# Half-block loop of an S5 layer: products of eigenvalue powers on VectorE four half blocks later, context rows of the fifth block earlier, two pair steps on VectorE

## The chip, the cores and the metric

The kernel runs on one core of a Trainium2 chip, as one launch. The time is device microseconds for one execution; each kernel is run several times, and the median counts. A profile is one further execution, recorded by the hardware profiler. Its *span* reaches from the first to the last instruction. Engines are called as in the profile's rows: PE (TensorE), PEld (its weight loads), DVE (VectorE), ACT (ScalarE), POOL (GpSimd), SP (SyncE, which here only issues transfers).

## The reference, cut to what matters

One layer (DEPTH is 1) of a backbone: an S5 mixer with a GLU over 1024 latent tokens behind a prefix of 256 context tokens, then a SwiGLU feed-forward, each with RMSNorm and adaLN. All is fp32. The part around the change is the S5 scan:

```python
lam_bar = jnp.exp(lam * jnp.exp(log_step.astype(F32))[:, None])
b_bar = ((lam_bar - 1.0) / lam)[..., None] * lax.complex(b_re, b_im)

def run(u, h0):
    bu = jnp.einsum('lgh,gnh->lgn', u.astype(F32), b_bar)
    bu = bu.at[0].add(lam_bar * h0)
    a = jnp.broadcast_to(lam_bar, bu.shape)
    _, h = lax.associative_scan(_linear_combine, (a, bu), axis=0)
    return jnp.einsum('lgn,ghn->lgh', h, c_mat).real, h[-1]

y_c, h_c = run(u_ctx, jnp.zeros(lam_bar.shape, lam_bar.dtype))
y_l, _ = run(u_lat, h_c)
```

There are 64 groups of 16 channels with 64 complex states each, and two directions. Only the latent rows of the result go on.

## The kernel before

**Chunks and half blocks.** The tokens are cut into chunks of T = 8: 32 chunks of context and 128 of latents, 160 in all. The S5 stage first works out what each chunk adds to the state. It does so in 16 *half blocks* (the loop `for hb in range(16)`, lines 699 to 757). Block b holds eight groups, and a half block is one block in one direction. For a half block the program makes an input matrix (`bl_make`: two products of the chunk's eigenvalue powers `LB` with B, on VectorE or, where `PMUL` says so, on GpSimd), adds the two (`bl_sum`: a DMA that accumulates, issued by GpSimd, from half block 4 on), turns the result on TensorE (`bl_tr`, line 443, with ScalarE's copy in line 446), and multiplies the tokens `U` with it (`sums`, line 584); ScalarE copies the chunk states into `STQ` (lines 590, 592 and 593). The work for later half blocks is spread over the loop: in half block hb, `bl_tr(hb + 2)`, `bl_sum(hb + 5)` and `bl_make(hb + 6)` are issued.

**What is interleaved.** The tokens of a block must be normalised and modulated before `sums` reads them: `rs_lat` (VectorE, table `RSL`), `u_act` (ScalarE, table `UACT`, line 497) and, for the context rows, `u_ctx` (GpSimd, table `UCTX`). `pair(hb - 1)` combines neighbouring latent chunks of the half block before, on GpSimd where `PPAIR` lists it and on VectorE otherwise. `ctx_tree` (VectorE, table `CTREE`) folds the 32 context chunks into one state by four doublings.

**Powers.** `PW` holds the powers 1 to 8 of the eigenvalues. Powers 1, 2, 4 and 8 are made early on VectorE; the other four are complex products, `pw_mul`. `pw_full` (line 386, copy in line 388) turns `PW` into `PWF`, which the products of C with the powers (`cl_ops`, GpSimd, from half block 12 on) read. `KD`, a small table, is made beside the first product.

**After the loop.** The last context tree is followed by `ctx_last` and `scan()`: 32 steps over two chunks and 63 over one, all on VectorE, each step dependent on the step before. GpSimd meanwhile makes the products of C, TensorE the convolution matrices and the outputs of what the scan has finished. Then come the GLU and the feed-forward, which fill the larger part of the time with TensorE.

**Order.** Nothing is scheduled by a planner: each engine executes its instructions in the order in which the Python code issues them (`manual_schedule`), and waits for others by semaphores. Tables such as `PPAIR` and `UCTX` therefore set the order. The helpers `tt`, `stt` and `ts` record all arithmetic, so its rows carry lines 77, 80 and 84 to 86; tiles and shapes tell them apart. In names, `ra`, `rw`, `rxa`, `rxc`, `ru`, `r` and `c` lie in SBUF; `lta`, `ltb`, `lbt`, `tq`, `ltc`, `pv`, `pw`, `pe`, `ut`, `xt` and `prow` lie in PSUM. `PW` and the states are in `ra`, the tokens in `ru`.

Of the kernel before, what the change touches and what calls it, by code (L numbers as in the profile page):

```python
# [24 lines left out]
G = 64  # L25
# [17 lines left out]
def s5_ffn_kernel(tc, a, out):  # L43
    nc = tc.nc
    V, S, E, PE, SY = nc.vector, nc.scalar, nc.gpsimd, nc.tensor, nc.sync
    ctx = ExitStack()
    with ctx:
# [5 lines left out]
        def view(reg, kb, shape, parts=P):  # L53
            off = int(round(kb * 256))
            n = int(np.prod(shape))
            v = reg[:parts, off:off + n]
            if len(shape) > 1:
                names = "abcdef"[:len(shape)]
                v = v.rearrange(f"p ({' '.join(names)}) -> p {' '.join(names)}",
                                **{k: d for k, d in zip(names, shape)})  # L60
            return v
# [3 lines left out]
        RA = region("ra", 80.5)  # L65
# [3 lines left out]
        RW = region("rw", 6)  # L69
# [6 lines left out]
        def tt(o, x, y, op, eng=V):  # L76
            eng.tensor_tensor(out=o, in0=x, in1=y, op=op)  # L77
# [263 lines left out]
        def pw_mul(o, x, y):  # L341

            m = x.shape[1]
            a_, b_ = (view(RA, kb, [m, 2, G]) for kb in (42, 43))
            yr, yi = (bc(bc(y[:, i], 1, 2), 1, m) for i in range(2))
            tt(a_, x, yr, MUL, E)
            tt(b_, x[:, :, ::-1], yi, MUL, E)
            tt(o[:, :, 0], a_[:, :, 0], b_[:, :, 0], SUB, E)
            tt(o[:, :, 1], a_[:, :, 1], b_[:, :, 1], ADD, E)

        LH = view(RXc, 0, [2, 3, G])
        SQ = [LS[:, 0], view(RXa, 7.25, [3, G]), LH[:, 0], LH[:, 1], LS[:, 1]]
# [326 lines left out]
            o = CL[q][:, ri, d]  # L679
            return [lambda: prod(0, o), lambda: prod(1, ct), add]  # L680

        PPAIR = (3, 5, 7, 8, 9, 11, 12, 13, 15)
        UACT = {1: (2, 0, 4), 2: (2, 4, 8), 3: (3, 0, 4), 4: (3, 4, 8)}
        UACT.update({6 + i: (4 + i // 2, 4 * (i % 2), 4 * (i % 2) + 4) for i in range(8)})
        UCTX = {1: 2, 3: 3, 6: 4, 7: 5, 9: 6, 11: 7}
        RSL = {0: 2, 1: 3, 3: 4, 5: 5, 6: 6, 8: 7}
        ADA1 = {0: (0, 1), 1: (2, 3, 4), 2: (5, 6, 7)}
        ADA2 = {10: 12, 11: 14, 12: 16, 13: 18, 15: 22}
# [9 lines left out]
        for hb in range(16):  # L698
# [38 lines left out]
                lb_psum(hb + 6)  # L737
            bl_sum(hb + 5)
            bl_make(hb + 6)
            if hb == 3:  # L740
                pw_mul(PW[:, 2:3], PW[:, 0:1], PW[:, 1])
                tt(KD.rearrange("p q g h -> p (q g) h"), bc(pat, 1, 8), bc(dcol, 2, HC), MUL, E)
            if hb == 4:
                pw_mul(PW[:, 4:6], PW[:, 0:2], PW[:, 3])
                pw_mul(PW[:, 6:7], PW[:, 2:3], PW[:, 3])
            if hb in (6, 8):
                pw_full(hb // 2 - 3)
            if hb == 9:
                cs_load(0)
            if hb == 11:  # L750
# [1009 lines left out]
```

## Time and profile before

| | us |
|---|---|
| median of three runs | 1024.25 (1023.15 to 1025.16) |
| profiled execution | 1022.42, of which span 1020.6 |
| TensorE busy over the span | 961.9 (94%) |
| VectorE busy over the span | 785.5 (77%) |
| GpSimd busy over the span | 766.5 (75%) |
| first and last start of the multiplications of `sums` (line 584) | 40.0 and 121.3 |
| all waits of TensorE on line 584 for GpSimd, 44 to 128 us | 2.6, one time |
| all waits of VectorE for ScalarE on line 593, 44 to 128 us | 5.3, two times |

How to read the rows that follow. A row of the order of time has the start and the duration in us, the engine, the line, the operation, the tile written and the tiles read, the shapes, and how many like instructions the row stands for. In brackets stands the time that the engine idled before it, and what ended that idling. A row of a group of instructions has its count behind an x. Starts are counted from the start of the span. DMA issues have a time to landing of their own.

### The profile page before, as it was taken

The numbers are of one execution on the slowest core, as the hardware profiler recorded it, in microseconds if no ns is written. First come the engines' busy times: TensorE is split into PE (matmuls) and PEld (weight loads), VectorE is DVE, ScalarE is ACT, GpSimd is POOL, SyncE is SP. The second block draws the span as 40 slices with busy tenths as digits, with TensorE's granted clock in tenths as the row PEclk, the third lists the DMA queues.
The fourth block names the chain that finished last, engine by engine and source line by source line (L and its number), as shares of the span: only waits on it lengthen the run. The fifth ranks groups of instructions, "written<-read, shape, count | busy, mean of one in ns | idle before, by whom it ended". The sixth has DMA issues, their size and how long they took to land. (4 is left out here: it accounts for less than half of the span.)

```text
span 1020.6 us, 18545 instructions
## 1 busy us (share of the span) xinstructions
PE 961.9 (94%) x6988; PEld 771.8 (76%) x6988; DVE 785.5 (77%) x1642; ACT 436.5 (43%) x854; POOL 766.5 (75%) x590
## 2 busy tenths in 40 slices
PE   5987798779999999999999999999999999999996
PEld 1466423668999987878888888888888888888885
DVE  7979799994365777997958768585958778686987
ACT  5477622234454663523334343424343343324337
POOL 5799899991682548979786877778686877777674
PEclk9999999989999999999999999999999999999999
DMA  9764997323612021011212112121212111121205
GB/s 335 276 139 91 298 341 231 91 74 89 227 61 83 2 104 62 22 42 42 83 41 74 39 45 62 42 73 52 73 42 82 39 40 58 42 73 52 73 22 165
DMA packets 48546, 98.95 MB, mean 97 GB/s; under 512 B 4285, under 2 KB 18877, under 8 KB 47177
## 3 DMA queue, kind: packets, MB, share of 16 engines
q1 hardware_dynamic: 43272, 86.64, 25.9%
q0 software_dynamic: 2016, 7.34, 3.8%
q10 hardware_dynamic: 3168, 3.79, 1.1%
q8 instruction: 55, 0.90, 0.4%
q14 instruction: 35, 0.28, 0.1%
HBM read 84.25 MB, written 6.17 MB: 89 GB/s over the span
## 5 line engine op out<-in xcount | busy, mean ns | idle before, releaser
L77 POOL TENSOR_TENSOR c<-rxc,c 128x512 fp32r<-128x512 f32 x128 | 170.0, 1342 | 55.6 <-ACT c L1227 53.7
L1286 PE MATMUL ut<-ra,c 128*128 128x512 f32 x400 | 155.8, 390 | 0.5 <-ACT ra L1227 0.3
L1287 PE MATMUL ut<-ra,c 128*128 128x512 f32 x400 | 155.7, 389 | 0.3 <-DVE ra L77 0.3
L1288 PE MATMUL ut<-ra,c 128*128 128x512 f32 x400 | 155.7, 389 | 0.0
L1227 ACT CAST c<-rxc 128x512 fp32r<-128x512 f32 x128 | 79.0, 622 | 146.4 <-PE xt L1568 51.8
L1568 PE MATMUL xt<-c,c 128*128 128x512 f32 x540 | 129.7, 389 | 0.0
L77 DVE TENSOR_TENSOR ru<-ru,xt 128x1024 f32<-128x1024 f32 x90 | 107.8, 1216 | 12.9 <-PE xt L1568 9.1
L1568 PEld LDWEIGHTS xt<-c,c 128*128 128x128 f32 x540 | 101.4, 188 | 21.0
L77 DVE TENSOR_TENSOR ru<-ut,ru 128x512 f32<-128x512 f32 x98 | 67.2, 686 | 42.4 <-PE ut L1288 36.9
L1286 PEld LDWEIGHTS ut<-ra,c 128*128 128x128 f32 x400 | 75.1, 188 | 16.7 <-ACT ra L1227 0.8
L1287 PEld LDWEIGHTS ut<-ra,c 128*128 128x128 f32 x400 | 75.1, 188 | 16.2 <-issue 0.6
L1288 PEld LDWEIGHTS ut<-ra,c 128*128 128x128 f32 x400 | 75.1, 188 | 15.9 <-POOL c L77 0.3
L77 POOL TENSOR_TENSOR c<-rw,c 128x512 fp32r<-128x512 f32 (+1 forms) x29 | 39.8, 1372 | 37.3 <-ACT c L1227 36.6
L77 POOL TENSOR_TENSOR c<-ru,c 128x512 fp32r<-128x512 f32 (+1 forms) x39 | 58.0, 1487 | 9.3 <-ACT c L1227 4.9
L1288 PE MATMUL ut<-c,c 128*128 128x512 f32 x160 | 62.4, 390 | 1.3 <-POOL c L77 1.3
L1287 PE MATMUL ut<-c,c 128*128 128x512 f32 x160 | 62.3, 389 | 0.0
L1286 PE MATMUL ut<-c,c 128*128 128x512 f32 x160 | 62.2, 389 | 0.0
L77 POOL TENSOR_TENSOR rxc<-rxc 128x512 f32<-128x512 f32 x40 | 60.9, 1523 | 1.6
L1568 PE MATMUL ut<-c,c 128*128 128x512 f32 x216 | 51.9, 389 | 0.0
L584 PE MATMUL pv<-ru,c 128*64 128x160 f32 x512 | 43.7, 312 | 7.3 <-POOL ru L77 2.6
L77 DVE TENSOR_TENSOR pe<-pe,ru 128x256 f32<-128x256 f32 x64 | 27.4, 429 | 29.5 <-ACT pe L1127 17.4
L77 DVE TENSOR_TENSOR ru<-ru,ut 128x512 f32<-128x512 f32 x76 | 47.3, 680 | 0.3
(427 smaller groups left out, 2568.2 us busy)
## 6 DMA issues: line engine op xcount, KB each, us to landing
c<-in_ada_w SPq DMA_DIRECT2D x46, 256.0 KB
rxc<-in_w SPq DMA_DIRECT2D x38, 256.0 KB
rxc<-in_w SPq DMA_DIRECT2D x19, 512.0 KB
ru<-in_w SPq DMA_DIRECT2D x11, 512.0 KB
rw<-in_w SPq DMA_DIRECT2D x11, 512.0 KB
ra<-in_ada_w SPq DMA_DIRECT2D x10, 512.0 KB
ra<-in_ada_w SPq DMA_DIRECT2D x18, 256.0 KB
ru<-in_xT SPq DMA_DIRECT2D x4, 1024.0 KB
```

Of the source, the lines that this page charges most:

```text
L77: eng.tensor_tensor(out=o, in0=x, in1=y, op=op)
L584: PE.matmul(pv[64 * (i % 2):64 * (i % 2) + 64, ri, c0:c0 + 160], w[:, i, 64 * ri:64 * ri + 64], U[:, 8 * b + 4 * j + i], start=True, stop= ...
L1227: S.copy(o[0], x)
L1286: PE.matmul(pu, wh, bh, start=start, stop=False)
L1287: PE.matmul(pu, wh, bl, start=False, stop=False)
L1288: PE.matmul(pu, wl, bh, start=False, stop=stop)
L1568: PE.matmul(pd, w[:, cs_], b, start=j in (1, 2, 4) and n == 0, stop=n == 2, skip_group_check=j not in (1, 2, 4))
```

## The change

Three things in the half-block loop are different.

`pw_mul`, the complex product of powers, is issued on VectorE (`V`) instead of GpSimd (`E`). Its two scratch tiles move from `ra` to one in PSUM (`LTb`) and one in SBUF (`RW`). The three calls come four half blocks later, 7 and 8 instead of 3 and 4, and `pw_full` comes in half blocks 9 and 10 instead of 6 and 8; `KD` goes along to half block 7 and stays on GpSimd.

The context rows of the fifth block (`u_ctx(4)`) are issued in half block 5 instead of 6.

Pair steps 8 and 12 leave the list for GpSimd, so VectorE executes them.

```diff
@@ def pw_mul(o, x, y):
             m = x.shape[1]
-            a_, b_ = (view(RA, kb, [m, 2, G]) for kb in (42, 43))
+            a_, b_ = (t[:, :128 * m].rearrange("p (m r n) -> p m r n", m=m, r=2) for t in (LTb, view(RW, 0, [256])))
             yr, yi = (bc(bc(y[:, i], 1, 2), 1, m) for i in range(2))
-            tt(a_, x, yr, MUL, E)
-            tt(b_, x[:, :, ::-1], yi, MUL, E)
-            tt(o[:, :, 0], a_[:, :, 0], b_[:, :, 0], SUB, E)
-            tt(o[:, :, 1], a_[:, :, 1], b_[:, :, 1], ADD, E)
+            tt(a_, x, yr, MUL, V)
+            tt(b_, x[:, :, ::-1], yi, MUL, V)
+            tt(o[:, :, 0], a_[:, :, 0], b_[:, :, 0], SUB, V)
+            tt(o[:, :, 1], a_[:, :, 1], b_[:, :, 1], ADD, V)
...
-        PPAIR = (3, 5, 7, 8, 9, 11, 12, 13, 15)
+        PPAIR = (3,5,7,9,11,13,15)
...
-        UCTX = {1: 2, 3: 3, 6: 4, 7: 5, 9: 6, 11: 7}
+        UCTX = {1: 2, 3: 3, 5: 4, 7: 5, 9: 6, 11: 7}
...
-            if hb == 3:
+            if hb == 7:
                 pw_mul(PW[:, 2:3], PW[:, 0:1], PW[:, 1])
                 tt(KD.rearrange("p q g h -> p (q g) h"), bc(pat, 1, 8), bc(dcol, 2, HC), MUL, E)
-            if hb == 4:
+            if hb == 8:
                 pw_mul(PW[:, 4:6], PW[:, 0:2], PW[:, 3])
                 pw_mul(PW[:, 6:7], PW[:, 2:3], PW[:, 3])
-            if hb in (6, 8):
-                pw_full(hb // 2 - 3)
+            if hb in (9, 10):
+                pw_full((9, 10).index(hb))
```

How the engines' lists change, at three places. The first is on VectorE, at the end of half block 7: the two rows at the top are the last of a context tree, the row of `ru` is the scaling of block 7's tokens.

```order
 L77 TENSOR_TENSOR ra<-ra,ltb 128x16x2x8
 L77 TENSOR_TENSOR ra<-ra,lbt 128x16x2x8
+L77 TENSOR_TENSOR ltb<-ra 128x128
+L77 TENSOR_TENSOR rw<-ra 128x128
+L77 TENSOR_TENSOR ra<-ltb,rw 128x64 x2
 L77 TENSOR_TENSOR ru<-ru,ltb 128x8x128
```

The first product of powers stands ahead of the scaling of block 7. Its two multiplications read `ra` twice.

The second place is on VectorE too, from half block 8 to 9: the rows of `c` are the two products of half block 14; behind the piece follow a context tree and the products of half block 15.

```order
 L77 TENSOR_TENSOR c_63<-c_63,lbt 128x1024
 L77 TENSOR_TENSOR c_66<-c_63,lbt 128x1024
+L77 TENSOR_TENSOR ltb<-ra 128x256
+L77 TENSOR_TENSOR rw<-ra 128x256
+L77 TENSOR_TENSOR ra<-ltb,rw 128x2x64 x2
+L77 TENSOR_TENSOR ltb<-ra 128x128
+L77 TENSOR_TENSOR rw<-ra 128x128
+L77 TENSOR_TENSOR ra<-ltb,rw 128x64 x2
+L77 TENSOR_TENSOR ltb<-ra,lta 128x256
+L77 TENSOR_TENSOR lbt<-ra,lta 128x256
+L77 TENSOR_TENSOR ra<-ra,ltb 128x32x2x4
+L77 TENSOR_TENSOR ra<-ra,lbt 128x32x2x4
```

The other two products of powers, and behind them pair step 8 (the last four rows), stand between the products of half block 14 and those of half block 15.

The third is on GpSimd, from half block 4 to 6: the rows of `c_64` and `rxc` are the two products of half block 10, the DMA is the sum of that half block, and the rows of `ru` are the context rows of the fifth block.

```order
 L77 TENSOR_TENSOR c_64<-c_63,c_65 128x1024
 L77 TENSOR_TENSOR rxc<-c_63,c_65 128x1024
-L77 TENSOR_TENSOR ra<-ra 128x256 x2
-L77 TENSOR_TENSOR ra<-ra 128x2x64 x2
-L77 TENSOR_TENSOR ra<-ra 128x128 x2
-L77 TENSOR_TENSOR ra<-ra 128x64 x2
+L77 TENSOR_TENSOR ru<-ru,r_60 128x8x32 x2
 L433 DMA c_64<-rxc 128x1024
-L77 TENSOR_TENSOR ru<-ru,r_60 128x8x32 x2
 L77 TENSOR_TENSOR rxc<-ra,r_60 128x256 x2
```

Two products of powers are gone from ahead of the DMA, and the context rows pass from behind it to ahead of it.

## The prediction, made before the result was known

> **What bounds the kernel now.** I first read the busy time by stretch, cut where the program's stages meet (columns: stretch, its length, then the busy time of TensorE, its weight loads, VectorE, ScalarE and GpSimd, the granted clock, DMA share, GB/s).
>
> ```profile
> 68.60:90.40 21.80, 18.07 (x180) 14.29 (x180) 20.12 (x55) 15.87 (x35) 21.17 (x33) 0.92 0.48 92
> 90.40:110.40 20.00, 15.70 (x160) 11.88 (x159) 18.87 (x49) 16.53 (x38) 19.53 (x26) 1.00 0.68 154
> 110.40:115.04 4.64, 3.57 (x43) 2.90 (x42) 0.00 (x1) 4.05 (x10) 4.56 (x6) 1.00 1.04 300
> 115.04:122.42 7.38, 6.05 (x69) 4.70 (x66) 5.28 (x20) 5.61 (x13) 7.30 (x9) 1.00 1.03 374
> 127.65:227.56 99.91, 83.63 (x1512) 48.12 (x1504) 97.77 (x509) 26.48 (x56) 96.86 (x66) 0.96 0.59 188
> ```
>
> From 127.65 to 227.56 us VectorE runs the serial scan without a gap (97.77 of 99.91 us), and the stages behind it start from its end. The scan starts 5.23 us after the last context tree, which starts at 122.42 when the loop's last states are copied. So this edit is worth what it does to that 122.42. Inside the loop GpSimd (21.17 of 21.80) and VectorE (20.12 of 21.80) are both full. Next I read VectorE's own order of time for what it still waits for:
>
> ```profile
> 115.04 0.43 DVE L77 TENSOR_TENSOR ltb<-ra,lta 128x256 f32<-128x256 f32 x1 [4.64 <-ACT ra L593]
> 120.20 0.43 DVE L77 TENSOR_TENSOR ltb<-ra,lta 128x256 f32<-128x256 f32 x1 [1.15 <-ACT ra L590]
> 122.42 0.43 DVE L77 TENSOR_TENSOR ltb<-ra,lta 128x256 f32<-128x256 f32 x1 [0.68 <-ACT ra L593]
> ```
>
> Those three gaps, 6.47 us, are all the slack VectorE has between 70 and 122 us apart from 0.4 us. TensorE waits in the same loop. The first of these rows is the wait for the context rows of the fifth block, the second the one for sum 14, the third the last transpose (half block 15); the fourth is ScalarE's copy of the last states, which ends the loop:
>
> ```profile
> 84.57 3.80 PE L584 MATMUL pv<-ru,c 128*64 128x160 f32 x32 [2.60 <-POOL ru L77]
> 109.81 1.06 PE L443 MATMUL pv<-r,c 128*128 128x128 f32 x8 [1.20 <-DMA c<-c]
> 114.40 1.09 PE L443 MATMUL pv<-r,c 128*128 128x128 f32 x8 [1.07 <-ACT ra L593]
> 122.12 0.27 ACT L593 COPY ra<-pv 128x128 f32<-128x128 f32 x1
> ```
>
> The last transpose reads a sum that an accumulating DMA finishes, issued on GpSimd once VectorE has made both products. The rows are VectorE's products, GpSimd's issue, and the landing that the query of that issue gives (minimum, median, maximum of one):
>
> ```profile
> 99.86 2.35 DVE L77 TENSOR_TENSOR c<-c,lbt 128x1024 f32<-128x1024 f32 x2 [0.20 <-ACT ra L590]
> 105.46 0.88 POOL L433 DMA_DIRECT2D c<-c  x1
> DMA to landing us min/median/max: 8.8/8.8/8.8
> ```
>
> 105.46 + 8.8 = 114.26: the transpose took the sum 0.14 us after it landed. Eight microseconds later (122.12 + 0.27 = 122.39) ScalarE has copied the last states. VectorE's products for half block 15 are thus one transfer away from the end of the loop.
>
> **What leaves GpSimd.** These rows, in order: the first product of powers, the other two, the context rows of the fifth block (they stay, earlier), pair step 8 and pair step 12 (two rows each).
>
> ```profile
> 68.61 1.84 POOL L77 TENSOR_TENSOR ra<-ra 128x128 f32<-128x128 f32 x4
> 78.08 4.27 POOL L77 TENSOR_TENSOR ra<-ra 128x256 f32<-128x256 f32 x8
> 82.91 1.60 POOL L77 TENSOR_TENSOR ru<-ru,r 128x256 f32<-128x256 f32 x2
> 99.10 1.30 POOL L77 TENSOR_TENSOR rxc<-ra,r 128x256 f32<-128x256 f32 x2
> 100.36 1.55 POOL L77 TENSOR_TENSOR ra<-ra,rxc 128x256 f32<-128x256 f32 x2
> 112.35 1.29 POOL L77 TENSOR_TENSOR rxc<-ra,r 128x256 f32<-128x256 f32 x2
> 113.60 1.52 POOL L77 TENSOR_TENSOR ra<-ra,rxc 128x256 f32<-128x256 f32 x2
> ```
>
> 1.84 + 4.27 + 2.74 + 2.73 = 11.6 us less on GpSimd. The fifth block's rows then end near 78 instead of 84.5 (6.1 us of products gone from ahead of them, and one accumulating issue of some 0.6), so TensorE's 2.60 us wait goes, and the 1.20 us for sum 14, which GpSimd issues sooner. I book none of this as gain: VectorE, which makes the products of half blocks 14 and 15, the context trees and the scan, has no wait there that these would shorten. The two small groups of transposing matmuls with their copies move from half blocks 6 and 8 to 9 and 10, same cost; at 10 they wait for VectorE's last product of powers (about 99 us), which eats the 2 to 3 us that TensorE had won.
>
> **What VectorE gets, without any disturbance.** A complex product of the same form stands early in the program, for one power and for two; the next instruction's start ends it.
>
> ```profile
> 27.87 0.28 DVE L77 TENSOR_TENSOR lta<-ra,ltb 128x128 f32<-128x128 f32 x1
> 28.66 0.95 DVE L535 RECIPROCAL ltb<-r 128x128 f32<-128x128 f32 x1
> 22.66 0.43 DVE L77 TENSOR_TENSOR lta<-ra,ltb 128x256 f32<-128x256 f32 x1
> 23.86 0.28 DVE L319 COPY ltb<-ra 128x128 f32<-128x128 f32 x1
> 102.13 0.42 DVE L77 TENSOR_TENSOR ltb<-ra,lta 128x256 f32<-128x256 f32 x1
> 103.58 0.42 DVE L77 TENSOR_TENSOR ltb<-ra,lta 128x256 f32<-128x256 f32 x1
> ```
>
> 0.79 us for one power, 1.20 for two: 2 x 0.79 + 1.20 = 2.78 for the three calls. A pair step takes 103.58 - 102.13 = 1.45; two are 2.90. Together 5.68 us, against 6.47 us of gaps. If nothing else happened, VectorE alone could begin the last context tree 0.79 us earlier, no more: that is the floor of the gain, -0.79.
>
> **What the new products meet.** The early products read one operand from PSUM (ltb). In the changed code both inputs of each multiplication, the power and the power that it is multiplied with, lie in SBUF (ra). The loop has no such row of VectorE beside a busy GpSimd, but the feed-forward stage has. First one with a PSUM operand, two with both operands in SBUF, and again one with PSUM; then GpSimd in the same microseconds.
>
> ```profile
> 615.51 0.68 DVE L77 TENSOR_TENSOR ru<-ru,ut 128x512 f32<-128x512 f32 x1
> 616.11 1.78 DVE L77 TENSOR_TENSOR c<-rxa,c 128x512 fp32r<-128x512 f32 x1
> 618.62 2.29 DVE L77 TENSOR_TENSOR ru<-ru,rxa 128x1024 f32<-128x1024 f32 x1
> 620.84 1.21 DVE L77 TENSOR_TENSOR ru<-ru,xt 128x1024 f32<-128x1024 f32 x1
> 616.05 1.29 POOL L77 TENSOR_TENSOR c<-rxc,c 128x512 fp32r<-128x512 f32 x1 [1.42 <-ACT c L1227]
> 618.54 1.29 POOL L77 TENSOR_TENSOR c<-r,c 128x512 fp32r<-128x512 f32 x1 [1.20 <-ACT c L1227]
> ```
>
> 1.78 instead of 0.68 and 2.29 instead of 1.21: each took about 1.1 us more, and each ends as if it had begun when GpSimd's instruction, started just ahead, was done. In the Trainium skill, "SBUF — State Buffer", section "Who interferes with whom", says this as a rule: a VectorE instruction with two SBUF inputs and a GpSimd instruction that reads SBUF exclude each other for the whole instruction, while one SBUF input contends with nothing; the trace agrees, with those 1.1 us. By that rule each of the six new multiplications waits for at most one GpSimd instruction; without it they would take what they take alone.
>
> The moved pair steps have a PSUM operand in every instruction, as the 0.42 us rows beside a full GpSimd do, so I add nothing to them. There are six multiplications with two SBUF inputs. Where they fall:
>
> ```profile
> 89.98 2.33 POOL L77 TENSOR_TENSOR c<-c,c 128x1024 f32<-128x1024 f32 x1
> 91.96 2.31 POOL L77 TENSOR_TENSOR rxc<-c,c 128x1024 f32<-128x1024 f32 x1
> 85.23 2.35 DVE L77 TENSOR_TENSOR c<-c,tq 128x1024 f32<-128x1024 f32 x2 [0.19 <-issue]
> 90.39 1.22 DVE L77 TENSOR_TENSOR ru<-ru,ltb 128x1024 f32<-128x1024 f32 x1
> ```
>
> VectorE's list is unchanged up to 90.39, where the first product (half block 7) is put in. GpSimd, now early, must wait for VectorE's products of half block 12 (85.23 row, done by 87.50) before it issues that sum; after it come its two products of half block 13, some 2.0 us each, from about 88.1 to 92.1. So one of the two multiplications at 90.39 has to sit out the second of them: the call ends near 93.1 rather than 91.18, +1.9 us (bounds 0, if the two miss each other, and 2.4). The other two calls, in half block 8, have four multiplications beside pair steps and context rows of some 0.65 to 0.8 us an instruction: 0 to 2.6 us, of which I take 1.0, because GpSimd stands still for part of that time. Sum +2.9, between 0 and 5.0; less than nothing is excluded, as a multiplication isn't shorter than alone. Behind these calls on VectorE stand the scaling of block 7, the context trees and the products of half blocks 14 and 15.
>
> **The sum.** Two roads lead to 122.42, and the later one counts.
> VectorE's own queue: -0.79 + 2.9 = +2.1 us (-0.8 to +4.2).
> The transfer: the products of half block 15 come 2.78 + 1.45 + 2.9 = 7.1 us later on VectorE; they ended by 102.2, so now at 109.3. GpSimd issued at 105.46, so the issue is 3.9 us late. In GpSimd's queue the context rows of block 7, pair step 11 and the first products of C wait behind it; with 11.6 us of its work gone GpSimd is ahead there and loses idle time only. For the landing the bounds are the 8.8 us above, shared with sum 14 and the weight loads, and the two accumulations that had loads alone beside them (minimum 6.4, median 7.2, maximum 7.9):
>
> ```profile
> DMA to landing us min/median/max: 6.4/7.2/7.9
> ```
>
> With 7.5 the sum lands at 116.9 against the 114.40 at which it was taken: +2.5 us (6.4: +1.4; 8.8: +3.8). The later road gives +2.5. Behind it GpSimd's and TensorE's work beside the scan shifts by no more than this, so it passes to the end. The profiled run took 1022.42 us with a span of 1020.6; it becomes 1024.9. The median of the runs, 1024.25, lies 1.83 above the profiled one; on that scale the forecast is 1024.25 + 2.5 = 1026.8 us.
>
> **Rivals.**
> (1) The multiplications slip between GpSimd's instructions and lose under 1.5 us in all. Then VectorE's queue gives -0.8 to +0.7, and the products of half block 15 end at 106.4 to 107.9, so that their sum lands 6.4 to 7.9 later at 112.8 to 115.8, no later than +1.4. Time 1023.5 to 1025.7, middle 1024.6. For it: GpSimd is ahead and idle more often. Against it: the 2.0 us products at 88.1 to 92.1 lie right across 90.39.
> (2) Faster: GpSimd, not VectorE, sets the loop's pace. Then the removed 2.60 us wait of TensorE and 1.20 us at sum 14 come through, up to -3.8 us; a middle of -2.6 gives 1021.7. For it: GpSimd's 21.17 busy of 21.80 us. Against it: to gain over 0.79 VectorE would have to do its longer list in less time. It decides only if VectorE's 5.68 us are under 4.4.
> (3) Sum 15 is caught behind the weight loads, which now start with it, since the first ones overwrite what VectorE's late copy of half block 15 reads. If landing takes 10 us or more, the transpose comes at 119.3 or later: +4.9, 1029.2. For it: 8.8 was seen already, with such loads beside it. Against: sum 14 is out of the way by then.
> (4) The change does nothing but shift waits, which is (1) with its middle at zero.
>
> **How the numbers follow.** The forecast's case (+1.4 to +3.8) gets 0.52, rival (1) with (4) 0.25, (3) 0.14, (2) 0.09. Two tenths of a per cent, about what a measurement can tell from no change, is 2.05 us. Of the forecast's case 0.46 lies above it and 0.06 below: slower 0.46 + 0.14 = 0.60, same 0.25 + 0.06 = 0.31, faster 0.09. The likeliest case's own range is 1025.6 to 1028.1. The range of 1023.4 to 1029.2 leaves out the faster case, the lowest edge of rival (1) and the far half of rival (3).
>
> **What will show it.** Right, if the first product of powers on VectorE, near 90.4, shows a multiplication of 1 us or more, where 0.3 is its own time; if VectorE's products for half block 15 end near 109 and GpSimd stands waiting for them; if the gap before the tree of half block 14 (4.64) is gone; and if the last context tree starts near 125 with the scan's length unchanged. TensorE's 2.60 us wait should be gone in any case. Wrong, if the six multiplications take 0.3 to 0.4 us each (rival 1), if the last tree starts before 121.6 (rival 2), or if the loop ends as now and the time moves behind the scan.

## The result, and the profile after

| | before | after |
|---|---|---|
| median of five runs each, us | 1024.21 (1023.15 to 1025.16) | 1033.83 (1033.50 to 1035.10) |
| ratio, 95% interval | | 1.0096 [1.0085, 1.0107] |
| span of the profiled execution, us | 1020.6 | 1031.5 |

The changed kernel is 9.6 us slower, where 2.5 were forecast. First the busy time by stretch of the changed kernel (columns as in the prediction: stretch, length, TensorE, its weight loads, VectorE, ScalarE, GpSimd, granted clock, DMA share, GB/s), cut at the events that the prediction followed:

```profile
68.60:90.80 22.20, 20.60 (x194) 16.61 (x196) 20.04 (x54) 16.06 (x37) 16.78 (x20) 0.86 0.55 104
90.80:96.20 5.40, 1.51 (x16) 0.98 (x10) 5.37 (x4) 4.82 (x13) 5.32 (x7) 0.94 0.34 64
96.20:105.80 9.60, 7.04 (x48) 5.97 (x48) 9.20 (x16) 4.05 (x9) 5.57 (x9) 0.68 0.63 143
105.80:114.00 8.20, 7.18 (x66) 5.79 (x66) 7.66 (x22) 4.82 (x12) 0.61 (x1) 0.80 0.31 82
114.00:124.23 10.23, 5.46 (x56) 4.03 (x55) 9.81 (x32) 6.79 (x16) 9.58 (x11) 0.93 0.81 213
124.23:133.35 9.12, 8.30 (x72) 7.31 (x72) 4.41 (x18) 5.58 (x13) 4.83 (x6) 0.70 0.85 225
138.57:238.50 99.93, 84.01 (x1500) 47.35 (x1496) 97.77 (x508) 26.65 (x56) 93.85 (x64) 0.97 0.57 187
```

The scan lasts 99.93 us, as before (99.91); it starts 10.9 us later, and the span is 10.9 us longer. The whole loss lies in the loop. The second row is the place to look at: in 5.40 us VectorE is busy throughout and finishes four instructions. In the fourth, GpSimd, one of the two full engines before, works 0.61 of 8.20 us. VectorE's order of time, around the products of powers and at the end of the loop:

```profile
90.80 5.16 DVE L77 TENSOR_TENSOR ltb<-ra 128x128 f32<-128x128 f32 x1
95.87 0.28 DVE L77 TENSOR_TENSOR rw<-ra 128x128 f32<-128x128 f32 x1
...
102.04 0.42 DVE L77 TENSOR_TENSOR ltb<-ra 128x256 f32<-128x256 f32 x1
102.37 0.42 DVE L77 TENSOR_TENSOR rw<-ra 128x256 f32<-128x256 f32 x1
...
103.35 0.30 DVE L77 TENSOR_TENSOR ltb<-ra 128x128 f32<-128x128 f32 x1
103.56 2.21 DVE L77 TENSOR_TENSOR rw<-ra 128x128 f32<-128x128 f32 x1
...
111.59 2.35 DVE L77 TENSOR_TENSOR c<-c,lbt 128x1024 f32<-128x1024 f32 x2 [0.20 <-ACT ra L592]
...
131.13 0.43 DVE L77 TENSOR_TENSOR ltb<-ra,lta 128x256 f32<-128x256 f32 x1 [3.75 <-ACT ra L590]
...
133.35 0.43 DVE L77 TENSOR_TENSOR ltb<-ra,lta 128x256 f32<-128x256 f32 x1 [0.69 <-ACT ra L593]
```

The first six rows are the multiplications with both inputs in SBUF. Four take their own time. The first takes 5.16 us instead of 0.28, the last 2.21: 4.88 + 1.93 = 6.8 us in which VectorE counts as busy and does nothing. The row at 131.13 shows the end of the loop: VectorE, done with everything else, waits 3.75 us for states that come of sum 15. So the transfer, not VectorE's own queue, ends the loop. GpSimd in the same microseconds:

```profile
88.62 0.88 POOL L433 DMA_DIRECT2D c<-c  x1 [5.11 <-ACT ra L590]
89.23 2.33 POOL L77 TENSOR_TENSOR c<-c,c 128x1024 f32<-128x1024 f32 x1
91.22 2.31 POOL L77 TENSOR_TENSOR rxc<-c,c 128x1024 f32<-128x1024 f32 x1
93.20 0.68 POOL L77 TENSOR_TENSOR r<-r 128x128 f32<-128x128 f32 x1
93.56 1.56 POOL L77 TENSOR_TENSOR rxc<-ra,r 128x256 f32<-128x256 f32 x2
94.81 1.91 POOL L77 TENSOR_TENSOR ra<-ra,rxc 128x256 f32<-128x256 f32 x2
...
102.75 0.88 POOL L433 DMA_DIRECT2D c<-c  x1 [3.87 <-PE pv L584]
103.36 1.59 POOL L77 TENSOR_TENSOR rxc<-ra,r 128x256 f32<-128x256 f32 x2
104.75 1.65 POOL L77 TENSOR_TENSOR ra<-ra,rxc 128x256 f32<-128x256 f32 x2
...
114.49 0.88 POOL L433 DMA_DIRECT2D c<-c  x1 [8.09 <-DVE ltb L77]
```

The first multiplication came in the middle of the first of these GpSimd products and got through at 95.7 us, after the rest of that product, the second product, the small one behind it, both multiplications of a pair step and the first of its two additions. Only there does GpSimd wait for something, since the second addition reads what the first one wrote. The last one, at 103.56, again got through between two such additions. GpSimd then stands 8.09 us before it can issue sum 15. The waits of 5.11 and 3.87 us bear the names of ScalarE and TensorE, but each of the three issues starts 0.55 to 0.64 us after VectorE's products of its half block end (87.98, 102.12 and 113.94), so I read all three as waits for VectorE. TensorE:

```profile
96.68 1.98 PE L386 MATMUL pv<-ra,r 128*64 128x256 f32 x8 [3.30 <-DVE ra L77]
106.31 1.98 PE L386 MATMUL pv<-ra,r 128*64 128x256 f32 x8 [2.59 <-DVE ra L77]
124.23 1.94 PE L443 MATMUL pv<-r,c 128*128 128x128 f32 x8 [4.49 <-DMA c<-c]
```

It waits for the late products of powers, 3.30 and 2.59 us, and 4.49 us for sum 15, taken 124.23 - 114.49 = 9.74 us after its issue. From the kernel before to the changed one, with the prediction between:

| us | before | predicted | after |
|---|---|---|---|
| products of half block 15 done on VectorE | 102.21 | 109.3 | 113.94 |
| sum 15 issued | 105.46 | 109.4 | 114.49 |
| sum 15 taken by TensorE | 114.40 | 116.9 | 124.23 |
| last context tree starts | 122.42 | 124.9 | 133.35 |

### The profile page after: what moved, and what is told of

The parts are those of the page before. It is cut to its first block, busy times and chain, and to the rows that moved or that the text cites. A ratio compares the mean times of both kernels' runs of the same rounds, so it can differ in the third digit from the quotient of the medians.

```text
span 1031.5 us, 18543 instructions
## 1 busy us (share of the span) xinstructions
PE 968.8 (94%) x6988; PEld 778.3 (75%) x6988; DVE 802.8 (78%) x1662; ACT 436.5 (42%) x854; POOL 755.5 (73%) x570
## 5 line engine op out<-in xcount | busy, mean ns | idle before, releaser
L77 POOL TENSOR_TENSOR c<-rw,c 128x512 fp32r<-128x512 f32 (+1 forms) x29 | 42.1, 1452 | 37.9 <-ACT c L1227 37.3
L77 POOL TENSOR_TENSOR c<-ru,c 128x512 fp32r<-128x512 f32 (+1 forms) x39 | 54.8, 1405 | 9.3 <-ACT c L1227 4.9
L584 PE MATMUL pv<-ru,c 128*64 128x160 f32 x512 | 47.3, 336 | 2.2 <-ACT ru L497 1.0
```

The costliest lines, as they stand in the source:

```text
L584: PE.matmul(pv[64 * (i % 2):64 * (i % 2) + 64, ri, c0:c0 + 160], w[:, i, 64 * ri:64 * ri + 64], U[:, 8 * b + 4 * j + i], start=True, stop= ...
```

## The experiments

Two theories stood at the start. Theory A: the held multiplications are most of the loss. The rival: the longer queue on VectorE and the late transfer of sum 15 are, and the held time is hidden in them. Each experiment that gives a ratio has its own runs of the kernel before on the same chip.

### One input of the multiplications in PSUM

```diff
+        yq = LTb[:, 384:512].rearrange("p (r n) -> p r n", r=2)
-            yr, yi = (bc(bc(y[:, i], 1, 2), 1, m) for i in range(2))
+            yr, yi = (bc(bc(yq[:, i], 1, 2), 1, m) for i in range(2))
...
             if hb == 7:
+                V.tensor_copy(yq, PW[:, 1])
...
             if hb == 8:
+                V.tensor_copy(yq, PW[:, 3])
```

> The changed kernel, but the power that is multiplied with is first copied to PSUM (two small copies on VectorE), so each new multiplication has one SBUF input instead of two. Theory A (the two multiplications of 5.16 and 2.21 us wait for GpSimd because both inputs lie in SBUF): all six take 0.3 to 0.45 us, VectorE's products of half block 15 end near 107 instead of 113.9, the last context tree starts between 122 and 125, time 1024 to 1026.5. Rival B (VectorE's longer list, 5.7 us more on a full engine, and what waits for it, cost the 9.6 us by themselves): the two long rows may shrink, but the time stays at 1032 or above.

Measured: 1026.96 us (1025.61 to 1027.84), ratio 1.0023 [1.0009, 1.0037], a little above theory A's range. The two rows of VectorE's order of time that were 5.16 and 2.21 us:

```profile
90.77 0.29 DVE L77 TENSOR_TENSOR ltb<-ra,ltb 128x128 f32<-128x128 f32 x1
...
99.37 0.29 DVE L77 TENSOR_TENSOR rw<-ra,ltb 128x128 f32<-128x128 f32 x1
```

With one input in PSUM no multiplication is held, though GpSimd has the same products under way (from 88.87 to 93.17 us). Some 7 of the 9.6 us are the two held multiplications and what follows from them.

### One part of the change at a time

The changed kernel without the two other parts leaves the products alone:

```diff
-        PPAIR = (3,5,7,9,11,13,15)
+        PPAIR = (3, 5, 7, 8, 9, 11, 12, 13, 15)
...
-        UCTX = {1: 2, 3: 3, 5: 4, 7: 5, 9: 6, 11: 7}
+        UCTX = {1: 2, 3: 3, 6: 4, 7: 5, 9: 6, 11: 7}
```

> Of the change only the products of powers on VectorE in half blocks 7 and 8 (and the turning in 9 and 10); context rows and pair steps as before. Theory A: most of the loss is here, 1030 to 1033.5, with multiplications of several us wherever GpSimd has instructions in a row. Rival B: 2.8 of the 5.7 us are here, so about half of the loss, 1028 to 1030, with no row above 1 us.

The same lines the other way round in the kernel before give the pair steps and the rows alone:

> Of the change only the context rows of the fifth block in half block 5 and pair steps 8 and 12 on VectorE; the products of powers stay on GpSimd in half blocks 3 and 4. Theory A: no new instruction has two SBUF inputs, TensorE's wait of 2.60 us at half block 8 goes, VectorE's 2.9 us fit into its gaps: 1021 to 1024.5. Rival B: 2.9 of the 5.7 us are here, so some of the loss, 1027 to 1030.

Measured: products alone 1031.21 us (1029.57 to 1032.56), ratio 1.0059 [1.0039, 1.0079]; pair steps and rows alone 1024.22 us (1023.17 to 1025.84), ratio 0.9995 [0.9983, 1.0008], no difference. The moved products lose alone, with two such records (5.13 and 2.35 us). The parts don't add up: 6.4 and -0.5 us apart by the medians, 9.6 together; I take it that the pair steps cost nothing in the gaps of the queue before, and their full time in a queue that is already late. Alone, the pair steps and rows turn TensorE's wait of 2.60 us for the rows into one of 1.83, and another, new one of 3.49 us for a sum whose issue GpSimd now puts behind the rows: a wait was exchanged.

### The products in other places of VectorE's list

```diff
-            bl_make(hb + 6)
-            if hb == 7:
+            if hb == 6:
                 pw_mul(PW[:, 2:3], PW[:, 0:1], PW[:, 1])
-                tt(KD.rearrange(
...
+            bl_make(hb + 6)
+            if hb == 7:
+                tt(KD.rearrange(
```

> The changed kernel with the same six multiplications, both inputs in SBUF, at other moments: the first call right ahead of VectorE's products of half block 12, the other two right ahead of those of half block 14, where GpSimd stood waiting for VectorE (5.11 and 3.87 us in the changed kernel). Theory A: GpSimd is idle at both, so all six take 0.3 to 0.45 us and the time is 1023.5 to 1027. Rival B: the same list is just as long, 1032 or above.

Measured: 1028.14 us (1026.20 to 1029.82), ratio 1.0030 [1.0017, 1.0043]. The first call met a GpSimd that stood still, and its multiplications took 0.29 and 0.28 us. The second met the pair step behind an issue, 2.20 and 0.94 us where 0.42 is alone, and the third the context rows, 0.79 where 0.28 is. So GpSimd did not stand still there, 2.8 us are held, and the time lies above theory A's range and below the rival's. Where the call stands decides what it loses.

### What holds VectorE through several instructions: trains

The prediction allowed for one GpSimd instruction for each multiplication. To see the rule by itself, GpSimd gets n multiplications ahead of the kernel before, while nothing else runs, and VectorE one multiplication that may start with the first of them. In the first set every one of a train wrote the same tile:

```diff
+        def train(n, chain=0, one=0, psum=0, m=1):
+            tt(g[1][:, 0:128], z[:, 0:128], lk.to_broadcast([P, 128]), MUL, E)
+            for i in range(n):
...
+                    tt(g[0], z, z, MUL, E)
+            for i in range(m):
+                tt(LTa[:, 128 * i:128 * i + 128], g[1][:, 0:128], LTb[:, 0:128] if psum else z[:, 128 * i:128 * i + 128], MUL)
```

> The kernel before, with nine short trains ahead of it while both engines have nothing else: GpSimd writes a tile, then issues n multiplications of 128x512 (about 1.0 us each) with nothing between them; VectorE waits for the tile alone and then does one multiplication of 128x128 of which both inputs lie in SBUF. n is 0, 1, 2, 4, 8; then 4 that each read the one before; 4 copies with one input; 4 beside a VectorE multiplication with one input in PSUM; 8 beside three VectorE multiplications. Theory A (VectorE gets in only when GpSimd's stream pauses): VectorE's record grows with n, to about 4 us at n = 4 and 8 us at n = 8, and is short where each instruction waits for the one before. Rival B (it waits for the one GpSimd instruction under way): never over 1.3 us, whatever n, and three in a row take up to 3. With an input in PSUM both expect 0.3 us. The extra part makes the kernel some 30 to 60 us longer; its time tells nothing else.

Measured: 1.12 us at n = 1, 2, 4 and 8, and also where each read the one before; 0.67 us beside copies of one input; 0.30 us with an input in PSUM; 3.35 us for three. That is one GpSimd instruction each, and theory A's form of it, "until the stream pauses", missed. But the trains had a gap of 0.08 us between instructions, since each waited for the write of the one before. So in the next set each wrote a tile of its own, with no wait:

```diff
+                o = RXc[:, 0:512] if same else free.pop()
...
+                    tt(o, z, z, MUL, E)
```

> Short trains ahead of the kernel before, as e6, with one difference: in e6 every GpSimd multiplication of a train wrote the same tile and so waited for the one before it (starts 1.11 us apart at 1.04 us each); here each of a train writes a tile of its own and waits for nothing. Order: 2, 3 and 5 multiplications beside one VectorE multiplication with both inputs in SBUF; 4 copies with one input; 3 multiplications beside three VectorE multiplications; 5 that all write one tile, as in e6. Theory A (VectorE gets in only where GpSimd waits for something): VectorE's records grow to about 2, 3 and 5 us in the first three, and are 1.1 us in the last. Rival B (one GpSimd instruction at most, as e6 showed for its trains): 1.1 us in all. For the copies A expects about 2.5 us and B 0.7.

Measured: 1.12 us at n = 2, 3 and 5, 0.67 us beside the copies, 3.21 us for three: one instruction each again. Next, operands like the kernel's, read repeatedly, and a later arrival:

```diff
+            tt(o, bc(z[:, 0:128].rearrange("p (g h) -> p g h", h=HC), 2, T),
+               bc(z[:, 128:192].rearrange("p (g s) -> p g s", s=T), 3, HC), MUL, E)
...
+            for i in range(late):
+                V.tensor_copy(LTb[:, 128:256], LTb[:, 0:128])
```

> Short trains ahead of the kernel before, now with operands like the kernel's own. The earlier trains held a VectorE multiplication for one GpSimd instruction, in the changed kernel it is held through five. Four trains: 3 GpSimd multiplications of plain 128x512 beside a VectorE multiplication whose second input is read twice over, as in the products of powers; 3 GpSimd multiplications of 128x1024 with both inputs read repeatedly, as in the products of a half block's rows (2.0 us each), beside a plain VectorE one; 2 of the same beside the VectorE one of the first train; 3 plain ones beside a plain VectorE one that arrives some 0.5 us later in the first. Theory C (VectorE's repeated input makes it lose each time): 3 us in the first, 1.1 or 2 us in the plain ones, 4 us in the third. Theory D (GpSimd's repeated inputs make it win each time): 1.1 us in the first, about 6 us in the second, 4 us in the third. Theory E (the moment of arrival decides): only the fourth long, about 2.5 us. Rival B (one instruction at most): 1.1, 2.0, 2.0 and under 0.8 us.

Measured: 0.92, 1.80, 1.80 and 0.29 us; each again what is left of one GpSimd instruction (rival B), and theories C, D and E missed. What the trains still lacked was seen in the rows of the kernel itself. Behind an issue of a transfer GpSimd's records overlap: 89.23 + 2.33 is 0.34 us past the start of the next at 91.22. Far from one they overlap by 0.06 us (119.41 + 2.03 against 121.38), in the trains by 0.04. So the last set issues an accumulating transfer just ahead:

```diff
+            wait_v()
+            if dma == "late":
+                E.dma_start(accs.pop(), z, accum_op=ADD)
+            tt(ld, z[:, 0:128], z[:, 128:256], MUL, E)
+            for i in range(n):
+                tt(free.pop(), z, z, MUL, E)
```

> Short trains ahead of the kernel before, with what the earlier trains lacked: GpSimd's issue of an accumulating transfer just ahead, as bl_sum's stands ahead of the instructions that held VectorE in the changed kernel. Behind such an issue GpSimd's rows overlap by 0.34 us (the next starts before the one before it ends), elsewhere by 0.04. Each train: GpSimd waits for VectorE, then (trains 2, 3 and 5) issues the transfer, writes a small tile, and does n multiplications of 128x512 with no wait among them; VectorE waits for the tile and does one multiplication with both inputs in SBUF. Train 1: n 5, no transfer. 2: n 2. 3: n 5. 4: n 4, with the transfer ahead of GpSimd's wait. 5: n 5, three VectorE multiplications. Theory F (behind an issue GpSimd keeps its next instruction at the door, and VectorE gets in only when GpSimd waits for something): 1.1 us in the first, about 2.2 in the second, 5.2 in the third, 1.1 in the fourth, 5.2 and then 0.3 each in the fifth. Rival B (one instruction whatever stands ahead): 1.1 us for each.

Measured, VectorE's order of time, one row for each train:

```profile
5.08 1.12 DVE L77 TENSOR_TENSOR lta<-ra,rw 128x128 f32<-128x128 f32 x1 [0.94 <-POOL ra L77]
...
11.89 2.11 DVE L77 TENSOR_TENSOR lta<-ra,rw 128x128 f32<-128x128 f32 x1 [5.50 <-POOL ra L77]
...
16.18 5.08 DVE L77 TENSOR_TENSOR lta<-rw 128x128 f32<-128x128 f32 x1 [1.99 <-POOL rw L77]
...
22.80 4.09 DVE L77 TENSOR_TENSOR lta<-rw 128x128 f32<-128x128 f32 x1 [1.35 <-POOL rw L77]
...
29.07 5.75 DVE L77 TENSOR_TENSOR lta<-rw 128x128 f32<-128x128 f32 x3 [1.99 <-POOL rw L77]
```

Without the transfer one multiplication is held for one of five; behind its issue for two of two (2.11), five of five (5.08), four of four (4.09), and of three in a row the first is held for all five and the others not (5.75). These are within 0.12 us of what theory F expected. Its 1.1 us for the fourth train missed, because the train did not do what it was built for: GpSimd came to its wait at 21.6 us, when VectorE had already released it at 21.5, and so did not stop. And what lets VectorE in need not be a wait: behind the third train's five the next entry of GpSimd's list is the issue of the fourth train's transfer, and VectorE got in there. GpSimd's rows of the third train:

```profile
14.78 0.87 POOL L159 DMA_DIRECT2D c<-rw  x1
15.39 0.75 POOL L77 TENSOR_TENSOR rw<-rw 128x128 f32<-128x128 f32 x1
15.81 2.31 POOL L77 TENSOR_TENSOR ra<-rw 128x512 f32<-128x512 f32 x2
17.80 3.29 POOL L77 TENSOR_TENSOR c<-rw 128x512 f32<-128x512 f32 x3
```

They overlap by 0.3 us, each starting before the one ahead has ended, as in the kernel. The long overlap and the long hold come together in every case here; that one makes the other is argued, not shown.

### A pause behind the issue, in the changed kernel

```diff
                 E.dma_start(bls(hb)[0], bls(hb)[1], accum_op=ADD)
+                if 12 <= hb < 15:
+                    tt(tiny[:, 0:1], cpk[:, 0:1], cpk[:, 0:1], ADD, E)
+                    tt(tiny[:, 1:2], tiny[:, 0:1], cpk[:, 0:1], ADD, E)
```

> The changed kernel with two tiny GpSimd additions (one element a partition, the second reads the first and so waits for it) behind the issues of sums 12, 13 and 14. Theory F: the pause ends the overlap, VectorE's multiplications are held by one GpSimd instruction each and the two long records (5.16 and 2.21 us) fall to under 1.5 us each; the time falls by most of what e1 gained: 1028.5 us (1027 to 1030.5). Rival (the pause comes too early to matter, or something else holds VectorE): both records as long as before, 1033 to 1035.

Measured: 1028.68 us (1027.59 to 1033.04), ratio 1.0040 [1.0026, 1.0054]. The profiled execution is the slowest of its five, and is read for the records only (its scan starts at 134.5 us, 4.1 earlier than in the changed kernel, but its span, 1031.2 us, is as long; what the loop won is lost behind the scan in this execution, and why is open):

```profile
90.94 1.35 DVE L77 TENSOR_TENSOR ltb<-ra 128x128 f32<-128x128 f32 x1
92.20 2.10 DVE L77 TENSOR_TENSOR rw<-ra 128x128 f32<-128x128 f32 x1
```

and beside them GpSimd's two products of a half block's rows:

```profile
90.10 2.03 POOL L77 TENSOR_TENSOR c<-c,c 128x1024 f32<-128x1024 f32 x1
92.09 2.06 POOL L77 TENSOR_TENSOR rxc<-c,c 128x1024 f32<-128x1024 f32 x1
```

Two additions of one element behind each of three issues take 5.1 us off the kernel, by the medians. The two rows are the first call's. GpSimd's records overlap by 0.04 us, and each of the two multiplications is held for the rest of one product: 1.07 + 1.82 = 2.9 us over their own 0.28, and no other is held at all. So one instruction for each is right where GpSimd has paused, as the prediction took it. The record of 5.16 us is down to 1.35 and that of 2.21 to 0.28, as expected; not expected was the second row, 0.28 us in the changed kernel, which now meets a product of its own.

This run also settles another rival, that the transfer itself, while it moves data, keeps VectorE out. Sum 12 was issued at 88.76 us and landed 4.5 us later, so both multiplications ran beside it and were held for one instruction each. In the changed kernel it landed 4.5 us after 88.62, at 93.1, and VectorE was held until 95.7.

### The transfer of sum 15 and the weight loads

In the changed kernel the first weight loads are issued at 111.45 us, into what VectorE's copy for half block 15 (line 428, at 111.09 us) has just read. Eight loads are issued by 114.8 us, so they are under way with sum 15; the ninth waits for it to land. The edit puts the buffers that sum 15 releases first in the list of load targets; the second version also puts the loads behind the transposes in the program.

```diff
-        stg = (stg + sl_ + (sx_ + stg[:4] + sl_) * 2 + (sx_ + stg[:4]) * 3)[:64]
+        stg = (stg[16:] + stg[:16] + sl_ + (sx_ + stg[:4] + sl_) * 2 + (sx_ + stg[:4]) * 3)[:64]
...
-        ADA2 = {10: 12, 11: 14, 12: 16, 13: 18, 15: 22}
+        ADA2 = {13: 18, 15: 22}
```

> The changed kernel, with the weight loads of the second matrix put into the buffers that sum 15 releases first, so that none of the 12 to 18 loads is under way while sum 15 is transferred (loads issued from about 112 us on in the changed kernel). Theory A (the late products are the cause, the transfer beside the loads makes it worse): sum 15 is issued where it was, near 114.5, but lands after about 5 us instead of 9.7; TensorE takes it near 119.5 and the loop ends 4 to 4.5 us earlier: 1029.5 us (1028.5 to 1031). Rival B (the loads don't matter to the transfer): landing again 9 to 10 us, time within 0.8 us of the changed kernel's 1033.8. Rival C: what is won at sum 15 is lost where the weights come later; landing short but time as in B.

> As e4, with the loads also placed behind half block 13's transposes in the program, so that they can't start before sum 15 has been read. In e4 the first load, which waits for sum 15 to land, was issued 4.7 us after sum 15's own issue. Theory A: sum 15 issued near 114.5, taken near 119.3 instead of 124.2, last context tree 4.5 us earlier than in the changed kernel: 1029.3 us (1028.3 to 1030.8). Rival C: the weights, 7 us later, make the first stage of the scan's TensorE work late enough to cost what is won: 1033 to 1034.

In the first, half block 15's transposes read weights in place of sum 15. Measured: 1033.72 us (1031.07 to 1035.59), ratio 1.0091 [1.0074, 1.0109], and 1037.47 us (1035.39 to 1039.40), ratio 1.0135 [1.0116, 1.0155]. In the first version, in order of time, the issue of sum 15 and the first load, which waits for it to land:

```profile
114.60 0.88 POOL L433 DMA_DIRECT2D c<-c  x1 [8.08 <-DVE ltb L77]
119.28 17.56 SPq L520 DMA_DIRECT2D c<-in_ada_w  x22
```

and TensorE in the second, at the transposes of half block 15 and at the product with the weights:

```profile
118.98 1.09 PE L443 MATMUL pv<-r,c 128*128 128x128 f32 x8 [1.07 <-ACT ra L593]
...
144.45 4.59 PE L531 MATMUL pm<-c,r 128*2 128x512 f32 x12 [2.34 <-DMA c<-in_ada_w]
```

Without loads beside it the sum lands 4.5 us after its issue in both versions, by the query of the issue, instead of 9.6; TensorE, in the second version, takes it at 118.98 when ScalarE lets it, 5.2 us earlier than in the changed kernel, and the scan starts at 133.5 (138.6 in the changed kernel). So the loads cost the transfer 5 us. Most of that is standing behind them: in the changed kernel only the loads' queue moves packets from 114.4 to 119.3 us (1.29 MB), and the 0.52 MB of the sum move between 119.3 and 123.4; in the first version its packets begin 1.4 us after the issue. But rival C came true as well, and further than expected: TensorE now waits for weights, GpSimd for TensorE, and the span is 2.0 us longer than the changed kernel's in spite of the earlier scan. A milder form, where loads start when sum 14 is taken, in the kernel before and in that with the power in PSUM:

```diff
+        stg = (stg[14:16] + stg[:14] + stg[16:] + sl_ + (sx_ + stg[:4] + sl_) * 2 + (sx_ + stg[:4]) * 3)[:64]
...
+        ADA2 = {12: 16, 13: 18, 15: 22}
```

> The kernel before with the first weight loads put into the buffers that sum 14 releases, so they start near 111 us instead of 102.6. Theory A (the loads share the transfer queues with sums 14 and 15): TensorE's wait of 1.20 us for sum 14 goes, the loop ends 1 us earlier, and the scan's TensorE work still has its weights in time (in e4 the loads started 17 us ahead of the scan at no cost, in e4b 12 us ahead at a cost of 7 us): 1023.2 us (1022.3 to 1024.5). Rival C (weights too late): 1026 to 1030.

> e1 (the changed kernel, one input of the products of powers in PSUM) with the loads of e15. Theory A: sum 15, issued near 108.4, is taken near 113.3 instead of 117.3, the loop ends 3 to 4 us earlier than in e1, the scan starts near 127 (127.9 in the kernel before): 1023.2 us (1022 to 1025). Rival C as in e15: 1026 to 1031.

Measured: 1024.27 us (1020.93 to 1028.13), ratio 1.0002 [0.9989, 1.0016]; and 1026.23 us (1022.70 to 1028.89), ratio 1.0018 [1.0005, 1.0031], against 1.0023 with the loads where they were. In the second TensorE takes sum 15 at 115.04 instead of 117.26 us and the scan starts at 128.3 instead of 130.7, and no time is won that can be told: TensorE waits 0.88 and 2.15 us for weights behind it. Sum 15 was expected to be taken at 113.3; it had landed 4.5 us after its issue at 108.36, but TensorE then waited for ScalarE.

### The products left on GpSimd, behind sum 15

If GpSimd's queue ahead of the sums were what sets the pace, the products could stay there and go behind the last issue.

```diff
-            if hb == 3:
+            if hb == 10:
                 pw_mul(PW[:, 2:3], PW[:, 0:1], PW[:, 1])
...
-            if hb == 4:
+            if hb == 10:
                 pw_mul(PW[:, 4:6], PW[:, 0:2], PW[:, 3])
...
-            if hb in (6, 8):
-                pw_full(hb // 2 - 3)
+            if hb == 11:
+                pw_full(0)
+                pw_full(1)
```

> The kernel before, with the products of powers left on GpSimd but moved behind the issue of sum 15 (half block 10), their scratch in the free row buffer, and both full-width copies of the powers at half block 11. Pair steps and context rows as before. Theory A (what delays the loop is GpSimd's queue ahead of the sums, and a product of powers on GpSimd costs VectorE nothing): sums 10 to 15 are issued up to 4.3 us earlier, TensorE's wait of 2.60 us for the context rows goes, VectorE's gap of 4.64 shrinks; loop end 2 to 4 us earlier: 1021.5 us (1020 to 1023.5). Rival B (GpSimd's queue behind sum 15 is as tight: the work put there makes pair 15 late, which the scan waits for): 1024 to 1028. Rival C (TensorE and ScalarE pace the loop anyway): 1023.5 to 1025.

Then the same with pair step 12 taken out of line 682's list; with the copies (`pw_full`) at half block 15 and no rows of the next stage (`CLAT`) in the loop; and that with pair step 6 put into the list:

```diff
-        PPAIR = (3, 5, 7, 8, 9, 11, 12, 13, 15)
+        PPAIR = (3, 5, 7, 8, 9, 11, 13, 15)
...
-            if hb == 11:
+            if hb == 15:
...
-        CLAT = {12: 1, 13: 1, 14: 2}
+        CLAT = {}
...
+        PPAIR = (3, 5, 6, 7, 8, 9, 11, 12, 13, 15)
```

> As e7, with the pair step of half block 12 on VectorE as well (1.45 us of VectorE, 2.7 us of GpSimd), behind the products for half block 15. Theory A: if GpSimd's queue behind sum 15 is tight in e7, this is up to 2.7 us faster than e7; if it is not, within 0.5 us of e7, or 1 us slower where VectorE's own queue ends last. 1021.5 us (1019.5 to 1024).

> As e7, with the full-width copies of the powers behind half block 15's sums (in e7 TensorE waited 3.92 and 2.31 us for GpSimd's products there) and the first rows of the next stage behind the loop. Theory A: the 6.2 us go, and what paces TensorE is the landing of sums 13 to 15: sum 15 issued near 104.2 and taken near 113 (114.40 before): 1023 us (1021.5 to 1024.5). Rival: the rows behind the loop make the next stage late: 1025 to 1028.

> As e11, with the pair step of half block 6 on GpSimd, which in e7 sat idle 4.23 us there waiting for VectorE's products for half block 12. Theory A (VectorE's queue sets when sums 12 to 15 are issued): all four 1.45 us earlier, 1021.5 us (1020 to 1023.5). Rival: GpSimd's 2.7 us for the step make sum 12 as late: no difference to e11.

In the last two the copies read powers over which the last states have been written, so what follows is computed from other numbers. Measured: 1029.96 us (1029.23 to 1030.82), ratio 1.0056 [1.0043, 1.0069]; 1029.44 us (1028.78 to 1032.47), 1.0055 [1.0043, 1.0068]; 1030.69 us (1028.89 to 1031.40), 1.0060 [1.0047, 1.0072]; 1029.91 us (1027.61 to 1031.30), 1.0053 [1.0041, 1.0066]. All four expectations of a gain missed. Sum 15 is issued about 1 us earlier than before in each (104.1 to 104.5 us), and nothing comes of it, since the late products stand in the way elsewhere. TensorE in the first, at the copies, which wait for GpSimd's products:

```profile
106.69 1.98 PE L386 MATMUL pv<-ra,r 128*64 128x256 f32 x8 [3.92 <-POOL ra L77]
110.99 1.98 PE L386 MATMUL pv<-ra,r 128*64 128x256 f32 x8 [2.31 <-POOL ra L77]
```

In the third that is gone, but now ScalarE, which copies states to where the powers lie, waits for GpSimd, and TensorE for ScalarE:

```profile
111.27 1.31 ACT L590 COPY ra<-pv 128x640 f32<-128x640 f32 x2 [1.99 <-POOL ra L77]
```

```profile
112.02 1.97 PE L443 MATMUL pv<-r,c 128*128 128x128 f32 x8 [4.62 <-ACT ra L590]
```

Pair step 12 or 6 made no difference that can be told. What an earlier sum 15 would be worth by itself stays open: none of the four had it without a new wait.

## Why the prediction fell short

**The direction and the road** were right: slower, by VectorE's multiplications with two SBUF inputs, and through the products of half block 15 and their transfer to the end of the loop, with the scan's length unchanged. The signs that it named came: a record over 1 us near 90.4, GpSimd waiting for VectorE's products, the gap of 4.64 us gone, TensorE's 2.60 us gone without gain. Two did not: VectorE's products for half block 15 ended at 113.94 instead of near 109, and the last tree started at 133.35 instead of near 125.

**The step that failed** is the term "each of the six new multiplications waits for at most one GpSimd instruction", +2.9 us with bounds 0 and 5.0. It measured 6.8 us, above its upper bound. Behind the issue of a transfer a multiplication here waited until GpSimd itself had to wait: the rest of one instruction and five more at 90.8 us, the rest of one and two more at 103.6. The step took its rule from the feed-forward stage, where each of GpSimd's two rows stood behind an idle time (1.42 and 1.20 us), and carried it to a place behind an issue. The rule of the Trainium skill that stood beside it ("SBUF — State Buffer", "Who interferes with whom": the loser is shut out for the whole of the other's instruction) agrees with every train without an issue (1.12 us where an instruction takes 1.04); behind an issue the runs show 5.08 us, and they decide. The sign was in a fence of the prediction: 89.98 + 2.33 is past 91.96. With a pause put in, the term is 2.9 us, and the kernel 1028.7 us, within the range. That the term is then the very number of the prediction is luck: all of it lies in the first call, for which 1.9 us was put in with 2.4 as the upper bound, since both of its multiplications met a product, and none in the other two calls, for which 1.0 was.

**The landing** was mis-sized, 7.5 us put in and 9.7 measured from the issue to TensorE's taking it (9.6 to the landing): +2.2. Rival (3), that the sum is caught beside the loads (10 us or more), had the mechanism and nearly the number; its argument against was true and did not help: sum 14, issued at 102.75, landed 4.9 us later, out of the way, but the loads alone make 4.5 into 9.6.

**The sum of the misses.** The last tree came 8.4 us later than predicted (133.35 against 124.9): 3.9 from the held multiplications, 0.7 elsewhere in VectorE's queue, 0.5 from the end of the products to the issue, 2.2 from the landing, and 1.1 from there to the tree, where the transposes took 1.94 us instead of 1.09; the granted clock was 0.70 in this stretch. The last of these wasn't foreseen.

**The rivals.** (1) and (4) fell with the 5.16 us record. (2), GpSimd as the pace, fell: in the changed kernel GpSimd waits 5.11, 3.87 and 8.09 us. The floor of the gain, VectorE's queue alone at -0.79 us, was not seen either: with no multiplication held the kernel is still 2.2 us slower than before [0.9 to 3.8], with 0.7 us of added copies in it and sum 15 waited for 3.30 us. No kernel of the study ran faster than the one before by more than the noise; the pair steps and rows alone run as fast.

## What to carry to other kernels

Before work goes from GpSimd to VectorE, look at where the inputs lie: an instruction with both in SBUF can be held by GpSimd, one with an input in PSUM was not. Where it must have both in SBUF, look for the issue of a transfer on GpSimd's queue ahead: the price here was all that GpSimd did up to its next wait or its next issue, and two tiny additions that make it wait brought that down to one instruction. Loads that start beside a transfer on the path can double its time to landing; but before they are moved away, see what waits for them.

## What the runs showed of the hardware

- Behind an accumulating transfer that it issues, GpSimd's records overlap by 0.3 us, until GpSimd stops for something; elsewhere by 0.04 to 0.06 us. In that state a VectorE multiplication with both inputs in SBUF, 0.30 us alone, took 2.11, 4.09 and 5.08 us beside two, four and five instructions of 1.0 us, and otherwise 1.12 us, whatever their number.
- GpSimd's copies with one input hold such a multiplication too (0.67 us), and the shapes of the inputs made no difference.
- Why an issue does this isn't shown. The Trainium skill ("Perfetto Trace Analysis", "DMA Instruction — SWDGE (GPSIMD)" and "GPSIMD Engine Instruction") says that two of GpSimd's processors prepare such a transfer, and that its processors aren't synchronised with each other outside single instructions. Processors that run behind one another from the issue on, until a wait lets them catch up, could give records that overlap by a fixed time; that would fit the rows, but no run here looked at single processors.
- An accumulating transfer of 512 KB landed 4.5 us after its issue alone, and 9.6 us with eight loads of 256 KB issued just ahead of it.
